# A sixth buffer for gated maps with eleven kept gelu results, a reordered mixing stage, and the next layer's first norm among the last V blocks

## The chip, the cores and the metric

One core of a Trainium2 chip runs the whole program. The metric is device time in microseconds, the median of several executions. TensorE is called PE here (its weight loads PEld), VectorE DVE, ScalarE ACT, GpSimd POOL, and SyncE SP; SP issues most of the transfers.

## What is computed

Two decoder layers over 512 tokens of 1024 channels, all float32. Each layer adds two sub-layers to x. The first mixes tokens with three groups of heads. The second, called PEER, picks for each token and each of eight heads 16 of 16384 experts and adds what they give:

```python
def reference(x, ...):
    for l in range(DEPTH):                       # DEPTH = 2
        xn = rms_norm(x, norm1_g[l])
        x = x + mixing_sublayer(xn, w_in[l], ..., w_out[l])
        xn = rms_norm(x, norm2_g[l])
        x = x + peer_ffn(xn, peer_wq[l], peer_keys[l], peer_u[l], peer_v[l])
    return x

# mixing: z = xn @ w_in, cut into three groups of heads
#   6 heads of stick-breaking attention (q, k normed), each head normed by out_g
#   6 heads of mLSTM (causal convolution and silu on q, k; input and forget gates), normed, times sigmoid(ml_o)
#   4 groups of spatial gating: gelu(u) * (w_s @ norm(gelu(v)) + b_s), normed;  result @ w_out
# PEER, for each token t:
sv, si = lax.top_k(scores, 16)                   # for each of the two half keys
best_s, best_p = lax.top_k(sums of pairs, 16);  gate = softmax(best_s);  idx = the pair's expert number
act = einsum('td,thkd->thk', xb, u_tab[ib])
y = einsum('thk,thkd->td', gelu(act) * gate, v_tab[ib])
```

## The kernel before

Tokens lie in four tiles of 128. PE works on float32 values split into a high and a low part (hi, lo), so that each product is three matmuls. A layer has these stages, and their times in layer 0 of the profiled execution are given for orientation.

**Mixing** (0 to about 330 us; function `mixing`). `norm_tiles` norms a tile of x (ACT squares and sums, `rsqrt_mean` takes Ln and Exp on ACT and some small DVE operations, DVE scales), and `to_channels` transposes it on PE and splits it into `xh` and `xl` on ACT and DVE. Then come the projections (`do_u`, `do_v`, `do_q`, `do_conv`, `do_mlv`, `do_og`), each with its weights loaded and split by `load_split`, and between them the heads (`sb_head`, `ml_head`), the spatial gating `sg_all`, the gate preparation `ml_prep`, the sigmoid of the output gate `og_sig`, the norm and transposition of the results `finish`, and the output projections `project_out`, which add to x. The order of the calls is written out (L570 to L614), but this part stands outside any manual schedule: a planner with its own costs may start an operation early where its operands and buffers are there. `act_set` preloads an activation table, and `tact` ties the activations that need it behind that load.

**PEER front** (to about 443 us; `peer_front`). Second norm, query projection, scores, and a top-16 search on DVE for each of the half keys. At its end `uprep(0)` splits the first block of u.

**Top-k, uact and gating** (443 to 823 us). From here the order on each engine is written by hand (`tc.manual_schedule`). The 16384 experts are 128 blocks of 128. For the first three tiles of tokens the kernel computes all of them: for each block e, `uact` multiplies u by x (24 matmuls, 128 x 384 each) and takes gelu. `uphase(e)` issues u_lo of block e+1 (DVE), the load of block e+4, u_hi of block e+2 (ACT) and then `uact(e)`. Results of blocks 0 to 59 (`NS`) are written to DRAM, the next ones (`NB`) are kept in SBUF. Beside that DVE runs `stage2`, the second top-k, tile by tile, and then the gating maps: for each of 24 batches of 16 tokens `make_maps(b, step)` makes two equality maps `oeq` (step 0; L900; two buffers) and three products `oag` of a map with a part of the gate (steps 1 to 3; L905; `AGB` = 5 buffers), and `quad(b, b4)` multiplies them on PE (12 small matmuls, L918) for four tokens at a time. `credit(w)` adds w to a balance and runs one `uphase` for each whole unit: `W_S` = 0.8 after each piece of `stage2`, `W_O` = 0.38 after each step of the maps. It stops at block `UB - 4` with `UB = NS + NB - 3`. The loop is

```python
for b in range(n_bat):
    for b4 in range(QB):
        quad(b, b4)
        make_maps(b + 1, b4)
        credit(W_O)
        gather((b * QB + b4) % 3 == 1)
```

The fourth tile (`NT - 1`) takes another way: `gather` fetches rows of u, then of v, by an indirect DMA on POOL and multiplies or adds them on DVE (L743, L754); there are 256 of these operations for a layer, spread over the gating and V stages.

**Tail and V stage** (823 to 1612 us). A short run of `uact` up to block `UB + 2`, then 128 V blocks: `vprep` multiplies gelu by the gate map and splits it and the block of v (wf, v_lo, wl on DVE; v_hi, wh on ACT), `vmm` adds 18 matmuls to six accumulators `ya`, which hold the result of three tiles. The remaining u blocks are interleaved, one to about two V blocks up to V block 120 (`UEND`). `spread(k, 252)` paces the gathers so that they end with step 252 of 256. After the last V block the six accumulators are added to x (L1042).

Layer 1 follows at once: its norm gains are loaded (L271), its first weights (L168), all four tiles are normed and transposed, and `do_u` takes the tiles in the order 0 to 3.

Of the kernel before, what the change touches and what calls it, by code (L numbers as in the profile page):

```python
# [17 lines left out]
P = 128  # L18
S = 512
# [22 lines left out]
NCH = TD // TC  # L42
GE = 4
GPAD = 128
NB = 13
NS = 60
UB = NS + NB - 3
W_S = 0.8
W_O = 0.38
G_R = 1  # L50
AGB = 5
UR = 3
G_B = 1
GBUF = 4
# [15 lines left out]
def trunk_kernel(ctx: ExitStack, tc: tile.TileContext, x, norm1_g, w_in, sb_qn_g, sb_kn_g, ml_conv_w,  # L70
# [56 lines left out]
    epoch = {"pre": None, "ops": []}  # L127
    no_sync = mybir.DependencyInfo(mybir.DependencyClass.NoSync, mybir.DependencyReason.SCHED_ONLY)

    def act_set(name):  # L130
        pre = nc.scalar.preload_act_table_set(name)
        for op in epoch["ops"]:
            tc.add_manual_dep(pre.ins, op.ins.name, no_sync, reason="table order")
        epoch["pre"], epoch["ops"] = pre, []

    def tact(out_ap, in_ap, func, **kw):
        op = nc.scalar.activation(out_ap, in_ap, func, **kw)
        tc.add_manual_dep(op.ins, epoch["pre"].ins.name, no_sync, reason="table order")
        epoch["ops"].append(op)
        return op  # L140

# [48 lines left out]
    def blocked(ap):  # L190
        return ap.rearrange("p (f c) -> p c f", c=ND)

    def to_channels(src, t, hi, lo, psp, perm=False):
        dst = slice(t * P, (t + 1) * P)
        cols = blocked(src) if perm else src.rearrange("p (c f) -> p c f", f=P)
        for d0 in range(0, ND, HALF):
            pt = psp.tile([P, S], F32, name="tr", bufs=1) if d0 else psp.tile([P, S], F32, name="zz", bufs=4)
            for d in range(HALF):
                nc.tensor.transpose(pt[:, d * P:(d + 1) * P], cols[:, d0 + d], ident)
            p3 = pt.rearrange("p (d t) -> p d t", t=P)  # L200
            sl = slice(d0, d0 + HALF)
            nc.scalar.activation(hi[:, sl, dst], p3, AF.Copy)
            nc.vector.tensor_sub(lo[:, sl, dst], p3, hi[:, sl, dst].bitcast(F32))
# [44 lines left out]
    def mixing(l, wst, fr, at, ps):  # L248
# [3 lines left out]
        with ExitStack() as yctx:  # L252
# [16 lines left out]
            if l == 0:  # L269
                load_x(0)  # L270
            nc.sync.dma_start(g1[:, :D], norm1_g[l][None, :].to_broadcast([P, D]))  # L271
            act_set(LOG_EXP)
            ws = [load_split(wst, w_in[l], C_UV, WG)]
            if l == 0:
                for t in range(1, NT):
                    load_x(t)
            ws.append(load_split(wst, w_in[l], C_UV + WG, WG))
            for t0 in range(NT):
                for t, xn in norm_tiles([t0], lambda: tmp("e", 1)[:, :D], lambda t: tmp("wt", 2)[:, :D],
                                        g1[:, :D]):  # L280
                    to_channels(xn, t, xh, xl, ps)
# [1 line left out]
            par, nm, bias_if, vn = load_params(l, ps)  # L283
            col = lambda key, i=0: par[:, nm[key] + i:nm[key] + i + 1]

            def natural(w, cw, evac):
                for t in range(NT):
                    pt = ps.tile([P, S], F32, name="mm", bufs=2)
                    mm3(pt[:, :cw], xp, w, lambda a, d: a[:, d, t * P:(t + 1) * P], lambda b, d: b[:, d, :])
                    evac(t, pt[:, :cw])  # L290

            def heads(pt, n):
                return pt.rearrange("p (h d) -> p h d", d=HD)
# [42 lines left out]
            def do_mlv(w):  # L336
                nc.gpsimd.memset(mlv[:, :, :, HD:HD + 1], 1.0)

                def evac(t, pt):
                    nc.vector.tensor_copy(mlv[:, t, :, :HD], heads(pt[:, :WM], HM))  # L340
                    nc.vector.tensor_add(ifn[:, t], pt[:, WM:].rearrange("p (a h) -> p a h", a=2), bias_if)

                natural(w, WM + 2 * HM, evac)

            def do_og(w):
                natural(w, WM, lambda t, pt: nc.scalar.activation(og[:, t, :], pt, AF.Copy))

            def do_u(w):
                natural(w, WG, lambda t, pt: nc.scalar.activation(uu[:, t, :], pt, AF.Copy))

            def do_v(w):
                natural(w, WG, lambda t, pt: nc.vector.tensor_copy(vv[:, t], heads(pt, GS)))
# [227 lines left out]
            do_conv(next_w(), 0)  # L580
            sb_head(1)
            do_conv(next_w(), 1)
            sg_all()
            sb_head(2)
            do_mlv(next_w())
            ml_prep()
            sb_head(3)
            sb_head(4)
            ml_head(0)
            sb_head(5)  # L590
            ml_head(1)
            do_og(next_w())
            og_sig()
            t_sb = mb.tile([P, 2, 3, S], F32R, name="yT_sb", tag="sqT")
            y_sb = (t_sb[:, 0], t_sb[:, 1])
            for c in range(3):
                finish(sbv, rsb, y_sb, c)
            ml_head(2)
            y_sg = (mb.tile([P, 2, S], F32R, name="yT_gh", tag="vv"),
                    yp.tile([P, 3, S], F32R, name="yT_gl", tag="sbv")[:, :2])  # L600
            u4 = uu.rearrange("p t (g d) -> p t g d", d=HD)
            for c in range(2):
                finish(u4, rsg, y_sg, c)
            project_out(y_sb, next_w(), 3, "mm", 2)
            ml_head(3)
            ml_head(4)
            project_out(y_sg, next_w(), 2, "mm", 2)
# [61 lines left out]
    def layer(l):  # L669
        with ExitStack() as pctx:  # L670
# [6 lines left out]
                    nc.sync.dma_start(uraw[e], peer_ut[l, e])  # L677

            def uprep_lo(e):
                if e in uraw:  # L680
                    src = uraw.pop(e)
                    nc.vector.tensor_sub(uT[e][1], src, uT[e][0].bitcast(F32))  # L682

# [9 lines left out]
            with ExitStack() as fctx:  # L693
                ps = fctx.enter_context(tc.tile_pool(name="ps_f", bufs=1, space=PSUM))
                wst = fctx.enter_context(tc.tile_pool(name="wst", bufs=1))
                mctx = ExitStack()
                fr = mctx.enter_context(tc.tile_pool(name="fr", bufs=1))
                at = mctx.enter_context(tc.tile_pool(name="at", bufs=1))
                mixing(l, wst, fr, at, ps)
                pr, xg, sbuf, svs, sis = peer_front(l, pctx, mctx, at, wst, ps, pools, uload)  # L700
                uprep(0)
            dr = pctx.enter_context(tc.tile_pool(name="dr", bufs=1, space=bass.MemoryType.DRAM))
            gd = dr.tile([NCH, P, NK * TC + GPAD], F32, name="gd")
            ge = dr.tile([NS, P, TD], F32, name="ge")
# [61 lines left out]
            def spread(k, n):  # L766
                if not left:
                    left.append(len(todo))
                gather(len(todo) - left[0] * max(0, n - k - 1) // n)

            with ExitStack() as bctx:
# [159 lines left out]
                        pace["credit"] -= 1  # L931

                with tc.manual_schedule():
                    uprep(1, lo=False)
                    uload(3)
                    for t in (NT - 1, *range(NT - 1)):
                        for _ in stage2(t):
                            credit(W_S)
                    casts = [f() for f in late]
                    credit(W_S)  # L940
                    for f in casts:
                        f()
                    tkctx.close()
                    with ExitStack() as octx:
                        oh = octx.enter_context(tc.tile_pool(name="oh", bufs=2))
                        stg = octx.enter_context(tc.tile_pool(name="stg", bufs=2))
                        for step in range(4):
                            make_maps(0, step)
# [7 lines that stand above are left out]
                u_tail = pace["e"]  # L956

            with ExitStack() as cctx:
# [26 lines left out]
                def vprep(k):  # L985
# [14 lines left out]
                    nc.vector.tensor_sub(wl, wf, wh.bitcast(F32))  # L1000
                    vT[e] = (wh, wl, vh, vl)

                def vmm(k):
                    e = order[k]
                    wh, wl, vh, vl = vT.pop(e)
                    for t in range(NT - 1):
                        tsl = slice(t * P, (t + 1) * P)
                        for half in range(2):
                            hs = slice(half * (D // 2), (half + 1) * (D // 2))
                            for i, (a, b) in enumerate(((wh, vh), (wh, vl), (wl, vh))):  # L1010
                                nc.tensor.matmul(ya[2 * t + half], a[:, tsl], b[:, hs],  # L1011
                                                 start=(k == 0 and i == 0), stop=(k == NK - 1 and i == 2))

                with tc.manual_schedule():
                    uprep_lo(u_tail + 1)
# [10 lines left out]
                    for k in range(NK):  # L1026
                        u_on = eu < NK and (k + 1) * (NK - NS - NB) >= (eu - NS - NB + 1) * UEND
                        vload(k + 2)
                        if u_on:
                            uload(eu + 4)  # L1030
                        vprep(k + 1)
                        spread(2 * k, 252)
                        if u_on:
                            uact(eu, ps, bufs=2)
                            uprep(eu + 2)
                            eu += 1
                        vmm(k)
                        spread(2 * k + 1, 252)
                for t in range(NT - 1):
                    for half in range(2):  # L1040
                        hs = slice(half * (D // 2), (half + 1) * (D // 2))
                        nc.vector.tensor_add(x_sb[:, t, hs], x_sb[:, t, hs], ya[2 * t + half])  # L1042

    for l in range(depth):
        layer(l)

# [35 lines left out]
```

## Time and profile before

| what | value |
|---|---|
| time, median of 3 executions (lowest to highest) | 3228.98 us (3225.39 to 3235.2) |
| the profiled execution, its own time | 3232.74 us |
| its span | 3231.0 us |
| mean granted clock of TensorE | 0.986 of full speed |
| busy in the span: PE, DVE, ACT, POOL | 3116.7, 2509.5, 1388.0, 681.5 us |
| DMA traffic | 748.49 MB, 232 GB/s on average, 320 GB/s in the V stage |

Busy times are those of one execution, in us or as a share of its span. PE's matmuls are pipelined, so a busy PE is not PE at its peak. "Idle before" is the time that an engine stood before an instruction, with the operation that ended that wait behind it. A line number stands for a line of the kernel; a helper's line is shared by all its callers, so the tile names tell them apart.

### The profile page before, as it was taken

To read this page: it belongs to the slowest core of one execution; us is meant where nothing else is said; L and a number is where in the kernel's file an instruction comes from. 1 tells how busy PE (TensorE), PEld (TensorE's weight loads), DVE (VectorE), ACT (ScalarE), POOL (GpSimd) and SP (SyncE) were. 2 spreads that over 40 slices of the span, in tenths; PEclk is the share of its full clock that TensorE was granted. 3 is DMA by queue.
4 is the path that set the end of the run, shared out by engine and by line. 5 is a ranking of instruction groups with operands and counts; after the bars stand their busy time and mean duration, and the time that the engine had idled before them with its cause. 6 is when DMAs were issued, how large, how long until landed. Compare 5 with 4: busy or idle time off the path is not lost.

```text
span 3231.0 us, 46311 instructions
## 1 busy us (share of the span) xinstructions
PE 3116.7 (96%) x17496; PEld 2776.7 (86%) x17496; DVE 2509.5 (78%) x4655; ACT 1388.0 (43%) x2002; POOL 681.5 (21%) x563
## 2 busy tenths in 40 slices
PE   8999999999999999999989999999999999999999
PEld 8877889998888888888887878899988888888888
DVE  4757889988677777877747578899886777778777
ACT  4553424566433333333355533345663333333333
POOL 1000000122233333333300000001212333333333
PEclk9999999999999999999999999999999999999999
DMA  4212325687999999999732123257879999999997
GB/s 141 68 33 61 102 70 176 232 291 264 337 331 324 324 332 316 334 330 323 252 107 67 34 60 101 75 186 242 289 262 322 328 329 321 332 318 336 328 324 264
DMA packets 329344, 748.49 MB, mean 232 GB/s; under 512 B 26404, under 2 KB 191328, under 8 KB 326048
## 3 DMA queue, kind: packets, MB, share of 16 engines
q1 hardware_dynamic: 233632, 401.76, 37.3%
q0 software_dynamic: 74752, 269.84, 23.9%
q10 hardware_dynamic: 20736, 73.93, 6.0%
q8 instruction: 137, 2.24, 0.3%
q14 instruction: 87, 0.71, 0.1%
HBM read 669.41 MB, written 76.02 MB: 231 GB/s over the span
## 4 chain that ended last, share of the span: by engine, by line
PE 85%; DVE 10%; ACT 3%; issue 2%; DMA 1%; SPq 0%; ACTq 0%; POOL 0%; DVEq 0%; POOLq 0%
PE y L1011 32%; PE act L714 26%; PE mm L187 13%; PE oh L918 4%; PE mm L533 3%; DVE u_lo L682 2%; DVE oag L905 1%; PE zz L367 1%; PE zz L653 1%; PE zz L467 1%; PE y L400 1%; PE y L478 1%; PE zz L392 1%; DVE bp L808 1%; DVE bp L805 1%
## 5 line engine op out<-in xcount | busy, mean ns | idle before, releaser
L714 PE MATMUL act<-xh,u_hi 128*128 128x384 f32 x2048 | 699.5, 342 | 6.4 <-ACT st L920 5.1
L714 PE MATMUL act<-xh,u_lo 128*128 128x384 f32 x2048 | 693.1, 338 | 11.2 <-DVE u_lo L682 11.2
L714 PE MATMUL act<-xl,u_hi 128*128 128x384 f32 x2048 | 693.0, 338 | 0.0
L1011 PE MATMUL y<-v_hi,wh 128*128 128x512 f32 x1536 | 599.9, 391 | 3.9 <-ACT wh L998 3.9
L1011 PE MATMUL y<-v_lo,wh 128*128 128x512 f32 x1536 | 599.6, 390 | 0.7 <-DVE v_lo L999 0.7
L1011 PE MATMUL y<-v_hi,wl 128*128 128x512 f32 x1536 | 598.7, 390 | 0.0
L997 ACT ACTIVATE v_hi<-v_raw 128x1024 fp32r<-128x1024 f32 x256 | 272.0, 1063 | 648.0 <-issue 575.5
L682 DVE TENSOR_TENSOR u_lo<-u_raw,u_hi 128x1024 fp32r<-128x1024 f32 x256 | 312.3, 1220 | 182.8 <-ACT u_hi L688 182.7
L999 DVE TENSOR_TENSOR v_lo<-v_raw,v_hi 128x1024 fp32r<-128x1024 f32 x256 | 312.9, 1222 | 160.8 <-ACT v_hi L997 160.8
L714 PEld LDWEIGHTS act<-xh,u_lo 128*128 128x128 f32 x2048 | 387.3, 189 | 13.6 <-DVE u_lo L682 13.3
L714 PEld LDWEIGHTS act<-xh,u_hi 128*128 128x128 f32 x2048 | 387.4, 189 | 11.4 <-ACT st L920 5.4
L714 PEld LDWEIGHTS act<-xl,u_hi 128*128 128x128 f32 x2048 | 387.2, 189 | 4.1
L740 POOL DMA_INDIRECT sbuf<-in_peer_u_dram,idx x128 | 170.8, 1334 | 1012.8 <-DVE sbuf L743 482.1
L717 ACT ACTIVATE gelu<-act 128x384 f32<-128x384 f32 x256 | 126.1, 492 | 521.7 <-PE act L714 521.6
L1011 PEld LDWEIGHTS y<-v_hi,wl 128*128 128x128 f32 x1536 | 289.2, 188 | 61.5 <-DVE wl L1000 0.7
L1011 PEld LDWEIGHTS y<-v_hi,wh 128*128 128x128 f32 x1536 | 288.8, 188 | 60.9 <-ACT wh L998 4.5
L1011 PEld LDWEIGHTS y<-v_lo,wh 128*128 128x128 f32 x1536 | 289.1, 188 | 57.0 <-DVE v_lo L999 1.3
L688 ACT ACTIVATE u_hi<-u_raw 128x1024 fp32r<-128x1024 f32 x256 | 271.7, 1062 | 37.0 <-ACT gelu L717 7.7
L740 POOL DMA_INDIRECT rows<-in_peer_u_dram,idx x128 | 165.5, 1293 | 365.9 <-DVE rows L743 354.1
L751 POOL DMA_INDIRECT sbuf<-in_peer_v_dram,idx x128 | 167.7, 1311 | 279.6 <-DVE x_sb L754 262.6
L920 ACT ACTIVATE st<-oh 128x512 f32<-128x512 f32 x192 | 198.6, 1141 | 46.6 <-PE oh L918 46.6
L751 POOL DMA_INDIRECT rows<-in_peer_v_dram,idx x128 | 159.3, 1245 | 280.0 <-DVE x_sb L754 246.4
(295 smaller groups left out, 5158.7 us busy)
## 6 DMA issues: line engine op xcount, KB each, us to landing
u_raw<-in_peer_ut_dram SPq DMA_DIRECT2D x256, 512.0 KB, 5.0
v_raw<-in_peer_v_dram SPq DMA_DIRECT2D x256, 512.0 KB, 6.5
gd<-st ACTq DMA_DIRECT2D x24, 2048.0 KB, 8.0
gt<-gd SPq DMA_DIRECT2D x64, 768.0 KB, 9.4
ge<-gelu ACTq DMA_DIRECT2D x120, 192.0 KB, 3.8
gelu_r<-ge SPq DMA_DIRECT2D x120, 192.0 KB, 6.1
w_raw<-in_w_in_dram SPq DMA_DIRECT2D x28, 768.0 KB, 4.4
w_raw<-in_peer_wq_dram SPq DMA_DIRECT2D x20, 768.0 KB, 5.5
```

The costliest lines, as they stand in the source:

```text
L187: nc.tensor.matmul(ps, a_sel(a[ah], d), b_sel(b[bh], d), start=(d == 0 and i == 0), stop=(d == n - 1 and i == 2))
L682: nc.vector.tensor_sub(uT[e][1], src, uT[e][0].bitcast(F32))
L688: nc.scalar.activation(uh, uraw[e], AF.Copy)
L714: nc.tensor.matmul(pa[:, :TD], a[:, d, :], b[:, d, :TD], start=(d == 0 and i == 0), stop=(d == ND - 1 and i == 2))
L717: nc.scalar.activation(gelu[e], pa[:, :TD], AF.Gelu_apprx_tanh)
L740: nc.gpsimd.indirect_dma_start(out=r, out_offset=None, in_=u_rows, in_offset=bass.IndirectOffsetOnAxis(ap=idx[:, p:p + 1], axis=0))
L751: nc.gpsimd.indirect_dma_start(out=r, out_offset=None, in_=v_rows, in_offset=bass.IndirectOffsetOnAxis(ap=idx[:, p:p + 1], axis=0))
L918: nc.tensor.matmul(pg[:, k, :], eq[:, 1, q, :, r], ag[i][:, q, :, r], start=(i == 0), stop=(i == 2))
L920: nc.scalar.activation(st[:, :, o:o + 4].rearrange("p i t -> p t i"), pg, AF.Copy)
L997: nc.scalar.activation(vh, vraw[e], AF.Copy)
L999: nc.vector.tensor_sub(vl, vraw.pop(e), vh.bitcast(F32))
L1011: nc.tensor.matmul(ya[2 * t + half], a[:, tsl], b[:, hs], start=(k == 0 and i == 0), stop=(k == NK - 1 and i == 2))
```

## The change

It has four parts. `AGB` goes from 5 to 6 and `NB` from 13 to 11, so that six products of maps can be in flight and 11 gelu results are kept. `uprep(1)` is moved from the beginning of the manual schedule to right behind `uprep(0)`, in the part that the planner orders, and with it its u_lo. In the mixing stage, `sg_all` comes after `ml_prep`, `finish` of the stick-breaking heads before `ml_head(1)`, `og_sig` after the first output projection, and the copy of the mLSTM values is made on ACT. Between the layers, the fourth tile of x, whose gathers now end with step 244 of 256, is normed for the next layer after V block 123 and transposed after V block 125; the table with Ln and Exp is loaded there and no more at the next layer's beginning; the accumulators are added to x tile by tile inside the last V block; and `do_u` of layer 1 begins with the fourth tile.

```diff
-NB = 13
+NB = 11
-AGB = 5
+AGB = 6
...
-    def act_set(name):
+    def act_set(name, manual=False):
         pre = nc.scalar.preload_act_table_set(name)
-        for op in epoch["ops"]:
+        for op in () if manual else epoch["ops"]:
             tc.add_manual_dep(pre.ins, op.ins.name, no_sync, reason="table order")
-        epoch["pre"], epoch["ops"] = pre, []
+        epoch["pre"], epoch["ops"], epoch["manual"] = pre, [], manual
...
-            act_set(LOG_EXP)
+            if l == 0:
+                act_set(LOG_EXP)
+            epoch["manual"] = False
...
-            for t0 in range(NT):
+            for t0 in range(NT if l == 0 else NT - 1):
...
-                    nc.vector.tensor_copy(mlv[:, t, :, :HD], heads(pt[:, :WM], HM))
+                    nc.scalar.activation(mlv[:, t, :, :HD], heads(pt[:, :WM], HM), AF.Copy)
...
-                natural(w, WG, lambda t, pt: nc.scalar.activation(uu[:, t, :], pt, AF.Copy))
+                natural(w, WG, lambda t, pt: nc.scalar.activation(uu[:, t, :], pt, AF.Copy),
+                        range(NT) if l == 0 else (NT - 1, *range(NT - 1)))
...
             do_conv(next_w(), 1)
-            sg_all()
             sb_head(2)
             do_mlv(next_w())
             ml_prep()
+            sg_all()
             sb_head(3)
             sb_head(4)
             ml_head(0)
             sb_head(5)
-            ml_head(1)
-            do_og(next_w())
-            og_sig()
             t_sb = mb.tile([P, 2, 3, S], F32R, name="yT_sb", tag="sqT")
             y_sb = (t_sb[:, 0], t_sb[:, 1])
             for c in range(3):
                 finish(sbv, rsb, y_sb, c)
+            ml_head(1)
+            do_og(next_w())
             ml_head(2)
...
             project_out(y_sb, next_w(), 3, "mm", 2)
+            og_sig()
             ml_head(3)
...
                 uprep(0)
+                uprep(1)
...
                 with tc.manual_schedule():
-                    uprep(1, lo=False)
                     uload(3)
...
+                def add_tile(t):
+                    for half in range(2):
+                        hs = slice(half * (D // 2), (half + 1) * (D // 2))
+                        nc.vector.tensor_add(x_sb[:, t, hs], x_sb[:, t, hs], ya[2 * t + half])
+
+                def ahead(k):
+                    t = NT - 1
+                    if k == NK - 10:
+                        nxt["g"] = vp.tile([P, D], F32, name="g_next", bufs=1)
+                        nc.sync.dma_start(nxt["g"], norm1_g[l + 1][None, :].to_broadcast([P, D]))
+                    elif k == NK - 5:
+                        act_set(LOG_EXP, manual=True)
+                        nxt["x"] = vp.tile([P, D], F32, name="x_next", bufs=1)
+                        for _ in norm_tiles([t], lambda: nxt["x"], lambda _: nxt["x"], nxt["g"]):
+                            pass
+                    elif k == NK - 3:
+                        to_channels(nxt["x"], t, xh, xl, ps, tags=(("act", 2), ("act", 2)))
...
+                        if k == NK - 1:
+                            add_tile(t)
...
-                        spread(2 * k, 252)
+                        spread(2 * k, 2 * NK - 12)
...
                         vmm(k)
-                        spread(2 * k + 1, 252)
-                for t in range(NT - 1):
-                    for half in range(2):
-                        hs = slice(half * (D // 2), (half + 1) * (D // 2))
-                        nc.vector.tensor_add(x_sb[:, t, hs], x_sb[:, t, hs], ya[2 * t + half])
-
+                        spread(2 * k + 1, 2 * NK - 12)
+                        if l + 1 < depth:
+                            ahead(k)
```

## Rows read from the trace of the kernel before

**Rows 1.** The page, busy us of each engine, share of span, instructions.

```profile
PE 3116.7 (96%) x17496; PEld 2776.7 (86%) x17496; DVE 2509.5 (78%) x4655; ACT 1388.0 (43%) x2002; POOL 681.5 (21%) x563
```

**Rows 2.** Stretches: length, busy PE, PEld, DVE, ACT, POOL, clock, DMA share, GB/s.

```profile
443.00:586.00 143.00, 134.20 (x736) 132.05 (x737) 136.81 (x462) 58.39 (x73) 4.06 (x4) 0.96 0.53 166
586.00:820.00 234.00, 217.92 (x1963) 210.56 (x1961) 207.45 (x213) 145.16 (x163) 48.55 (x31) 1.00 0.78 272
...
857.00:1610.00 753.00, 752.65 (x3614) 661.93 (x3614) 594.59 (x745) 270.46 (x363) 269.47 (x214) 1.00 0.92 320
```

**Rows 3.** Waits, whole span: who for whom, total us, times, longest us.

```profile
DVE oag L905 <- PE oh L918: 52.9, 38, 4.9
...
PE oh L918 <- DVE oag L905: 32.2, 28, 1.9
```

**Rows 4.** Timeline of PE in the gating stage: start, length, idle before.

```profile
656.07 0.73 PE L918 MATMUL oh<-oag,oeq 128*128 128x128 bf16 x10 [1.09 <-DVE oag L905]
...
675.63 0.73 PE L918 MATMUL oh<-oag,oeq 128*128 128x128 bf16 x10 [1.09 <-DVE oag L905]
...
820.03 2.93 PE L918 MATMUL oh<-oag,oeq 128*128 128x128 bf16 x48
```

**Rows 5.** Timeline of DVE in the same stretch of the gating stage.

```profile
654.79 1.23 DVE L905 TENSOR_TENSOR oag<-oeq,gateT 128x2048 bf16<-128x2048 bf16 x1 [1.27 <-PE oh L918]
655.94 2.35 DVE L900 TENSOR_TENSOR oeq<-iota_t,idxT 128x2048 bf16<-128x2048 bf16 x2
658.21 1.22 DVE L682 TENSOR_TENSOR u_lo<-u_raw,u_hi 128x1024 fp32r<-128x1024 f32 x1
659.34 1.22 DVE L743 SCALAR_TENSOR_TENSOR sbuf<-sbuf,xg 128x1024 f32<-128x1024 f32 x1
...
660.49 2.36 DVE L905 TENSOR_TENSOR oag<-oeq,gateT 128x2048 bf16<-128x2048 bf16 x2
```

**Rows 6.** Timeline of PE in the top-k stage, two of its stops.

```profile
453.12 0.69 PE L714 MATMUL act<-xh,u_lo 128*128 128x384 f32 x1 [4.79 <-DVE u_lo L682]
...
574.02 0.41 PE L868 MATMUL tr<-ident,ii 128*128 128x128 f32 x2 [1.62 <-DVE ii L852]
```

**Rows 7.** Timeline at the layer boundary: adds, weights, table, split, scaling, PE.

```profile
1609.22 2.73 DVE L1042 TENSOR_TENSOR x_sb<-x_sb,y 128x512 f32<-128x512 f32 x4 [1.43 <-PE y L1011]
...
1613.11 0.93 SPq L168 DMA_DIRECT2D w_raw<-in_w_in_dram  x2
...
1615.02 1.28 ACT L137 ACT_TABLE_LOAD   x1
1616.31 0.30 ACT L137 ACTIVATE rq_b<-rq_m 128x1 f32<-128x1 f32 x2
...
1619.07 1.04 ACT L173 ACTIVATE w_hi<-w_raw 128x1024 fp32r<-128x1024 f32 x1
...
1619.78 1.28 DVE L214 SCALAR_TENSOR_TENSOR wt<-x_sb,rs,sp 128x1024 f32<-128x1024 f32 x1
...
1621.16 1.09 PE L199 MATMUL zz<-ident,wt 128*128 128x128 f32 x4 [8.58 <-issue]
```

**Rows 8.** Stretches of the mixing stage and the layer boundary, as rows 2.

```profile
160.00:170.00 10.00, 7.72 (x32) 5.10 (x31) 7.80 (x18) 4.21 (x10) 0.00 (x0) 0.93 0.28 80
...
230.00:240.00 10.00, 7.72 (x41) 7.22 (x40) 6.55 (x11) 9.08 (x21) 0.00 (x0) 0.85 0.01 2
...
1612.60:1621.20 8.60, 0.04 (x1) 0.07 (x2) 2.96 (x10) 8.42 (x14) 0.14 (x2) 0.69 0.59 191
1621.20:1630.00 8.80, 7.09 (x32) 6.39 (x33) 6.07 (x16) 8.69 (x14) 0.00 (x0) 0.52 0.46 128
1630.00:1645.00 15.00, 12.75 (x104) 12.10 (x103) 8.31 (x12) 6.96 (x14) 0.00 (x0) 1.00 0.33 106
```

**Rows 9.** Groups by line, 185 to 260 (ACT) and 130 to 190 (DVE).

```profile
L154 ACT ACTIVATE sg<-og 128x384 f32<-128x384 f32 x4 | 2.1, 526 | 0.0
...
L543 DVE TENSOR_TENSOR vv<-vv,sgr 128x1024 f32<-128x1024 f32 x1 | 1.2, 1219 | 0.0
```

More of the change, by code (lines that the diff above doesn't have):

```diff
@@ L128, in trunk_kernel @@
     no_sync = mybir.DependencyInfo(mybir.DependencyClass.NoSync, mybir.DependencyReason.SCHED_ONLY)
-    def act_set(name):
+    def act_set(name, manual=False):
         pre = nc.scalar.preload_act_table_set(name)
-        for op in epoch["ops"]:
+        for op in () if manual else epoch["ops"]:
             tc.add_manual_dep(pre.ins, op.ins.name, no_sync, reason="table order")
-        epoch["pre"], epoch["ops"] = pre, []
+        epoch["pre"], epoch["ops"], epoch["manual"] = pre, [], manual
     def tact(out_ap, in_ap, func, **kw):
         op = nc.scalar.activation(out_ap, in_ap, func, **kw)
-        tc.add_manual_dep(op.ins, epoch["pre"].ins.name, no_sync, reason="table order")
+        if not epoch["manual"]:
+            tc.add_manual_dep(op.ins, epoch["pre"].ins.name, no_sync, reason="table order")
         epoch["ops"].append(op)
@@ L191, in blocked, with to_channels @@
         return ap.rearrange("p (f c) -> p c f", c=ND)
-    def to_channels(src, t, hi, lo, psp, perm=False):
+    def to_channels(src, t, hi, lo, psp, perm=False, tags=(("zz", 4), ("tr", 1))):
         dst = slice(t * P, (t + 1) * P)
@@ L196, in to_channels @@
         for d0 in range(0, ND, HALF):
-            pt = psp.tile([P, S], F32, name="tr", bufs=1) if d0 else psp.tile([P, S], F32, name="zz", bufs=4)
+            name, bufs = tags[d0 // HALF]
+            pt = psp.tile([P, S], F32, name=name, bufs=bufs)
             for d in range(HALF):
@@ L284, in mixing, with natural @@
             col = lambda key, i=0: par[:, nm[key] + i:nm[key] + i + 1]
-            def natural(w, cw, evac):
-                for t in range(NT):
+            def natural(w, cw, evac, tiles=range(NT)):
+                for t in tiles:
                     pt = ps.tile([P, S], F32, name="mm", bufs=2)
@@ L679, in uprep_lo @@
             def uprep_lo(e):
-                if e in uraw:
+                if e in uraw and e in uT:
                     src = uraw.pop(e)
@@ L1001, in vprep @@
                     vT[e] = (wh, wl, vh, vl)
+                def add_tile(t):
[14 more added lines that the diff above has]
+                        to_channels(nxt["x"], t, xh, xl, ps, tags=(("act", 2), ("act", 2)))
+                nxt = {}
                 def vmm(k):
```

## The prediction

> **What bounds the kernel now.** I read the page first, then the busy times by stretch, then the list of waits, then the order of instructions where a wait repeats. The page says that TensorE is busy for 96% of the span [rows 1], so a gain has to come out of the remaining 4%, or out of stretches in which its clock is low. The stretches show where those lie [rows 2]: in the V stage PE is busy for 752.65 of 753 us, so nothing can be won there and all PE work moved into it is paid in full. In the gating stage (586 to 820, its twin of layer 1 is alike) PE is idle for 16 of 234 us, while DVE is busy for 207. The list of waits names it [rows 3]: PE waits 28 times, 32.2 us in all, for a gate product (oag), and DVE waits 38 times, 52.9 us, for PE to give an oag buffer back. Each waits for the other, which is what too few buffers look like. The order on PE shows the rhythm [rows 4]: every second batch PE stops for 1.09 us in its first quad; from one stop to the next it is 19.56 us. On DVE the third product of the next batch is only made when PE has ended the batch before [rows 5].
>
> **The change part by part.** All sums are against the profiled execution, 3232.7 us with a span of 3231.0; the median of the timed runs, 3229.0, is 3.7 lower, and I carry the difference over to it unchanged.
>
> *Sixth map buffer.* With five buffers the third product of batch b+1 waits for the last quad of batch b. With six it waits for nothing that is recent. The next limit is oeq with two buffers: the first map of batch b+1 may start when quad 3 of batch b-1 has ended. From there DVE has to do two maps (2.27 us start to start), three products of 1.15, and its share of u_lo (1.13) and gather products (1.15) [rows 5]. Until PE needs the result, five credit calls of 0.38 pass, 1.9 uact blocks, and four quads; four quads take 2.93 us [rows 4] and a block 4.1 (two batches hold 8 quads and about 3 blocks: 19.56 - 1.09 - 5.9 = 12.6, by three). So PE has 2.9 + 1.9 x 4.1 = 10.7 us, DVE needs 2.27 + 3.45 + 1.9 x 1.13 + 1.33 x 1.15 = 9.4. DVE mostly comes in time; where only one block falls in between (about one batch in ten) it is 7.0 against 8.4 and PE waits 1.4. I leave 2.4 such waits, 3 us, in each layer: -32.2 + 6 = **-26**. Over two batches DVE has 17.9 us of work and PE 18.5, so the stage stays PE's, by 0.6 us.
>
> *Two fewer kept results (NB 13 to 11).* The cap on blocks in this stage falls from 66 to 64. 37 credit calls of 0.8 bring 29.6 blocks, then come four calls of 0.38 and one after each quad: the last block comes after quad 87 of 96 instead of quad 92. The two blocks go to the V stage (57 instead of 55 there), where PE pays the same 4.1 us: zero. Their DVE part, two u_lo, goes where DVE is busy 595 of 753 us [rows 2]: zero. But the last batch now has no block over it: PE has four quads (2.9 us), DVE from the release of oeq on 2.27 + 3.45 + 1.15 = 6.9, so PE waits about 3.9 us. Before, the last four quads ran without a stop [rows 4]. **+7.8** for two layers. If the clock falls after this wait too, about 3 us more a layer: idle PE at the layer boundary is followed by 8.8 us at a granted clock of 0.52 [rows 8], and this wait is half as long. I take none of it, and keep +6 as the bound.
>
> *uprep(1) ahead of the top-k stage.* PE's longest stop in that stage is 4.79 us for u_lo [rows 6]. The edit moves one u_lo to where DVE is less busy, but the next u_lo stands behind the same top-k work, and DVE is busy 136.8 of 143 us there [rows 2]. At 574 PE again waits for DVE (1.62 us) [rows 6], so whatever PE wins at the start it gives back there, except DVE's own saving of one operation: 1.13 us a layer, **-2.3**, at least 0, at most the full 9.6.
>
> *Next layer's first norm.* This counts once. Now PE ends V at 1612.6 and stands 8.58 us [rows 7]; then come 8.8 us at clock 0.52 with 1.7 us of gaps, and 2.25 us of gaps until 1645 [rows 8]. The adds of x are no part of it: four of them already run from 1609.22, under the last matmuls [rows 7]. The weights are asked for at 1613.11, when V's buffers come free, and ACT splits them at 1619.07 [rows 7]; tile 3 being ready in advance, PE waits for that load instead: 0.5 us to the issue, at most 6.0 to the split and I take 5 (ACT was busy too), 1.04 for the split, so 6.5 in place of 8.6. ACT loses its seven table loads of 1.28 us, 9.0 in all [rows 7], since one load now stands in the last V blocks; I count half of the 4 us of gaps for it. The clock falls either way. -2.1 - 2.0 = -4.1. The transposes of tile 3 move into V at their price: zero. In block 123 the norm's chain (square, Ln, Exp on ACT, 1.28 us of scaling on DVE [rows 7]) stands ahead of the preparation of a later block, which has the length of one V block to be ready in: 753 us less 55 uact blocks of 4.1 is 128 times 4.1. It has little to spare: +0.5, bounds 0 and 4.1. The norm weights are one more 512 KB on the SP queue among v loads, which are buffered three deep: zero. The gathers end four blocks earlier, 3% more of them per block, under DVE's 158 us of slack [rows 2]: zero. **-3.6**.
>
> The Trainium skill ("ScalarE: Activation LUTs", What ACT_TABLE_LOAD costs) gives a switch of set 1283 ns and a drain of about 1380 more. Here the activation behind a load starts 0.01 us after it [rows 7], so I see no drain; by the page the seven loads would be 18.6 us.
>
> *Mixing order.* finish of the stick-breaking heads comes before ml_head(1) and do_og, so its transposes have some 16 us of matmuls (do_og's 96 at 0.17, a 24th of a uact block) to hide in; now PE is idle for 2.3 us at 230 to 240 and its clock is 0.85 [rows 8]. sg_all goes behind ml_prep; now PE is idle for 2.3 us in 160 to 170 at 0.93 [rows 8]. og_sig goes behind the first projection, and the copies of mlv go from DVE to ACT; both engines are half idle. A planner orders this stage, so new stops can appear anywhere. At best both stops and their clock go, 4.6 + 2.2 = 6.8 a layer; at worst others replace them. I take 4 a layer, **-8**, bounds -14 and +8.
>
> Sum: -26 + 7.8 - 2.3 - 3.6 - 8 = **-32**: 3200.6 for the profiled execution, **3197** for the median.
>
> **The rivals.**
> DVE takes over the gating stage. It has 17.9 us of work in each 18.5; 5% slower operations make 18.8, and with 0.3 for uneven batches 19.1, 0.6 over PE, in 12 pairs of batches and two layers: +15, 3212. For it: DVE's load; against it: its 52.9 us of waiting are there to be used [rows 3]. The Trainium skill ("Perfetto Trace Analysis", Identifying the Most-Contended Engine) would judge PE by weight loads rather than matmuls: 210.6 us against DVE's 207.5 [rows 2], which makes this rival look nearer.
>
> The sixth buffer isn't the one that was missing: DVE then waits for oeq at the same place, the 26 us stay and the 7.8 are paid: -6, 3223. Against it: DVE's listed waits in this stage are all before oag, none before oeq.
>
> ACT's loads set the boundary: then all 9.0 us come off it and not 3.6: -5.4, 3192. For it: PE starts behind ACT's chain; against it: the weights' load ends late anyway. The rule of the skill above would make this still more.
>
> Slower: the new mixing order lays bare what it moves. og_sig is 16 activations of 0.52 us, 8.4 us, on ACT ahead of ml_head(3), and sg_all begins with three DVE operations of 1.22, 3.7 us, ahead of sb_head(3) [rows 9]. If PE has nothing else then, it stands 12.1 us a layer and loses about 6 more to the clock, as after the boundary [rows 8]: 36 in both, with the 8 not gained: -32 + 8 + 36 = +12, 3241. It outweighs the rest once two thirds of it are bare. Against it: around these places PE is busy nearly all the time, and projections are there to fill.
>
> **How the numbers follow.** Forecast 0.62 (3182 to 3209 by itself: the bounds of the mixing order and of the boundary, not all at once), DVE as the bound 0.14, ACT's loads 0.08, no effect 0.09, slower 0.07. A measurement of this kernel tells about 0.3%, 10 us, from no change. Faster by more than that: the forecast, DVE and ACT, 0.84; the same: 0.09; slower: 0.07. The range 3179 to 3216 takes in the first three, with the falling clock and the mixing bounds, and leaves out the last two.
>
> **What would show it.** PE's waits for oag fall from 28 to about five and DVE's busy share in the gating stage rises from 89% towards 95%; a new wait of about 4 us stands before the last batch; the first wait for u_lo comes one block later and is shorter, and the wait at the turn of tile 2 is longer; no table loads after the last V block, and PE idle of 6 to 7 us there; the 2.3 us stops at the stick-breaking finish are gone. I am wrong if the waits before quads stay, if V gets PE idle time, or if the mixing stage changes by more than 14 us.

## The result and the profile after

The changed kernel takes 3204.2 us (median of five; 3199.8 to 3212.8) where the kernel before, timed beside it, takes 3228.0: a ratio of 0.9933 with a 95% interval of 0.9918 to 0.9948, 0.7% faster. The forecast was 3197 us, with a range of 3179 to 3216. (One execution of a later run, g2, took 6182.6 us and stands in no figure below.) The profiled execution of the changed kernel has a span of 3206.5 us, against 3231.0.

The page, busy us of each engine (answers [rows 1]):

```profile
PE 3123.8 (97%) x17496; PEld 2782.4 (87%) x17496; DVE 2506.4 (78%) x4647; ACT 1383.3 (43%) x2004; POOL 677.6 (21%) x563
```

PE does the same 17496 matmuls, but is busy 7 us longer than before. So the span became 24.5 us shorter although matmuls took longer somewhere, and that is a matter of clock: the mean granted clock is 0.981, where it was 0.986. The list of waits, columns as in [rows 3]:

```profile
DVE oeq L906 <- PE oh L924: 20.5, 16, 3.1
PE oh L924 <- DVE oag L911: 11.5, 10, 2.0
...
PE tr L513 <- DVE dg L510: 4.3, 2, 2.2
```

PE's waits for gate products fall from 28 to 10 (forecast about five) and from 32.2 to 11.5 us; DVE no longer waits for an oag buffer at all, but for oeq, the next limit that the prediction named. The last line is new: a stop in the stick-breaking finish. Stretches, columns as in [rows 2]; 591 to 806 is the gating stage up to its last quad, the second line is the V stage:

```profile
591.00:806.00 215.00, 209.21 (x1937) 202.91 (x1936) 204.51 (x212) 144.20 (x162) 50.02 (x32) 0.99 0.82 293
840.00:1604.00 764.00, 763.73 (x3676) 672.41 (x3677) 601.96 (x756) 276.69 (x374) 267.05 (x214) 1.00 0.91 318
```

DVE is busy for 95% of the gating stretch (89% in [rows 2]), and PE idles 5.8 us of 215 where it idled 16 of 234. V stays full. Two thirds of the remaining waits stand at one place per layer, here on the timeline of PE:

```profile
800.26 0.23 PE L924 MATMUL oh<-oag,oeq 128*128 128x128 bf16 x1 [1.99 <-DVE oag L911]
801.39 0.22 PE L924 MATMUL oh<-oag,oeq 128*128 128x128 bf16 x1 [0.90 <-DVE oag L911]
802.53 1.71 PE L924 MATMUL oh<-oag,oeq 128*128 128x128 bf16 x17 [0.92 <-DVE oag L911]
```

That is the last batch, which has lost its U blocks: 3.8 us, forecast 3.9. The layer boundary, stretches as in [rows 8] and then the table loads on ACT's timeline from 1603 to 1622:

```profile
1604.90:1610.70 5.80, 0.08 (x2) 0.06 (x1) 3.08 (x14) 5.19 (x13) 0.14 (x2) 0.80 0.75 241
1610.70:1620.00 9.30, 9.30 (x62) 9.24 (x63) 8.85 (x13) 6.19 (x10) 0.00 (x0) 0.76 0.52 149
1620.00:1630.00 10.00, 9.59 (x80) 9.34 (x80) 2.82 (x5) 4.24 (x8) 0.00 (x0) 1.00 0.51 159
```

```profile
1608.77 0.20 ACT L137 ACTIVATE rs<-rq_b 128x1 f32<-128x1 f32 x1
...
1609.78 1.28 ACT L131 ACT_TABLE_LOAD   x1
1611.08 1.06 ACT L174 ACTIVATE w_hi<-w_raw 128x1024 fp32r<-128x1024 f32 x1
```

PE idles 5.72 us instead of 8.58 (forecast 6.5), has 0.4 us of gaps afterwards instead of 4.0, and 9.3 us at 0.76 instead of 8.8 us at 0.52. Of the seven table loads one is left here, for gelu; forecast was none. The mixing stage of layer 0, stretches:

```profile
230.00:240.00 10.00, 9.64 (x55) 7.39 (x54) 5.31 (x9) 6.79 (x13) 0.00 (x0) 1.00 0.34 107
240.00:250.00 10.00, 7.16 (x20) 4.61 (x20) 6.56 (x24) 4.36 (x16) 0.00 (x0) 0.65 0.00 0
250.00:260.00 10.00, 10.00 (x32) 7.04 (x31) 4.57 (x14) 2.41 (x8) 0.00 (x0) 0.50 0.00 1
260.00:270.00 10.00, 10.00 (x47) 7.88 (x46) 4.84 (x16) 2.73 (x9) 0.00 (x0) 0.82 0.01 2
```

The stop of [rows 8] at 230 to 240 has become one at 240 to 250, and behind it the granted clock is at the lower level (0.50 is 1.2 GHz) for some 20 us, through the second slice and into the third while PE is fully busy. The first U block of layer 0 starts at 446.85 instead of 443.52. The mixing stage thus lost time, where the forecast had -8.

### The profile page after: what moved, and what is told of

Read it like the earlier page. It is cut to its first block, busy times and chain, and to the rows that moved or that the text cites. A ratio compares the mean times of both kernels' runs of the same rounds, so it can differ in the third digit from the quotient of the medians.

```text
span 3206.5 us, 46330 instructions
## 1 busy us (share of the span) xinstructions
PE 3123.8 (97%) x17496; PEld 2782.4 (87%) x17496; DVE 2506.4 (78%) x4647; ACT 1383.3 (43%) x2004; POOL 677.6 (21%) x563
```

## The experiments

The theory after the result (A): the buffers and the boundary give more than forecast, and the new mixing order costs some 9 us through the clock. Rival: the terms of the prediction hold, and the missing 7 us are somewhere else. In what follows "old order" means the changed kernel with the mixing stage as it was.

**Buffers and cap by themselves.**

```diff
# e1_six_cap11, from the kernel before       # e2_cap11: the first line alone
-NB = 13
+NB = 11
-AGB = 5
+AGB = 6
```

> The kernel before with only the two sizes of the gating stage changed: six buffers for gated maps, 11 kept gelu results. Theory A, from the trace after: the gating stages lost 10.7 and 14.9 us beside the two U blocks that left each of them, the V stages gave 0.8 back, so this alone is worth about -25 us: 3203, nearly all of the change's gain. Theory B, the terms of the prediction: -26 + 7.8 = -18, so 3210, and the rest of the gain comes from the other edits.

> The kernel before with only the cap of kept gelu results lowered from 13 to 11; five buffers stay. Theory A, the prediction's term: the last block comes before quad 88 instead of 93, which opens waits of 3.9 us per layer, and the two U blocks moved among the V blocks cost nothing: +8, 3236. Rival: those two blocks, 4.3 us each, also covered the wait for a buffer in the gating stage; with five buffers every one of their microseconds is waited again, +17, 3245. Second rival: with five buffers the queue before the last blocks is no shorter than before, so nothing changes: 3228.

Measured: e1 3205.1 us, ratio 0.9927 (0.9913 to 0.9941); e2 3237.7, ratio 1.0030 (1.0021 to 1.0038). PE's and DVE's waits for each other, e2 first, then e1:

```profile
DVE oag L905 <- PE oh L918: 48.0, 34, 4.1
PE oh L918 <- DVE oag L905: 39.1, 34, 1.9
```

```profile
DVE oeq L900 <- PE oh L918: 16.7, 15, 2.4
PE oh L918 <- DVE oag L905: 11.4, 10, 2.0
```

The cap alone costs 9.3 us (forecast 7.8), of which 6.9 are waits. The sixth buffer on top of it is worth 32.5 (forecast 26). Its waits fall by 27.7 us; from the first quad to the first V matmul the two layers take 247.9 and 248.2 us in e1 against 264.0 and 265.5. The stage times decide for A: 16.1 and 17.3 us a layer, where the prediction's term is 13. By the median alone e1 lies 2 us above A's 3203 and 5 below B's 3210. In e2 the prediction's term for the cap fits, and its two rivals (3245 and 3228) don't.

**The preparation of block 1 ahead of the top-k stage.**

```diff
# h1_six_uprep, from e1
-                if e in uraw:
+                if e in uraw and e in uT:
...
 uprep(0)
+uprep(1)
...
-                    uprep(1, lo=False)
```

> Six buffers and the lower cap (3205.1) with the second U block's preparation moved ahead of the top-k stage; no other edit. Theory: the wait for u_lo at the second block falls from 4.79 to 3.08 us in layer 0 and as much in layer 1, and nothing else moves: -3, 3202. Rival: the wait comes back at a later block, 3205. With it, the old mixing order in the changed kernel (3194.4) differs from this by the next layer's first norm alone: -8 by the traces, -3.6 by the prediction.

Measured: 3205.6 us, ratio 0.9936 (0.9923 to 0.9950), against 3205.1 for e1: nothing. PE's timeline in e1, then in h1:

```profile
449.64 0.69 PE L714 MATMUL act<-xh,u_lo 128*128 128x384 f32 x1 [4.79 <-DVE u_lo L682]
...
570.54 0.41 PE L868 MATMUL tr<-ident,ii 128*128 128x128 f32 x2 [1.63 <-DVE ii L852]
```

```profile
452.98 0.69 PE L715 MATMUL act<-xh,u_lo 128*128 128x384 f32 x1 [3.08 <-DVE u_lo L682]
...
570.27 0.41 PE L869 MATMUL tr<-ident,ii 128*128 128x128 f32 x2 [1.62 <-DVE ii L853]
```

The stop is 1.7 us shorter, yet from the first U block to the first quad h1 takes 144.3 us and e1 143.8. The rival, that it comes back, fits. The stop at the turn of tile 2 is no longer than before (1.63 and 1.62), but the granted clock behind it differs, in e1 and then in h1:

```profile
570.00:580.00 10.00, 9.21 (x53) 9.00 (x54) 9.79 (x16) 2.72 (x4) 0.00 (x0) 1.00 0.39 121
```

```profile
570.00:580.00 10.00, 9.47 (x46) 9.26 (x47) 9.79 (x16) 2.25 (x3) 0.00 (x0) 0.83 0.36 111
```

That is 9.47 x 0.17 = 1.6 us of clock, about what the shorter stop had won; in layer 1 h1 has 0.83 as well (2170 to 2180) and e1 1.00. Where the clock stays up there, in f2 below, these stretches take 142.9 and 142.7 us, 1 us less than in e1 (143.8 and 143.9).

**The mixing order off, and alone.** e3_after_oldmix takes the hunk of the mixing stage and the copy on ACT out of the changed kernel; e4_mix_only puts just these into the kernel before.

> The changed kernel with the mixing stage in its old order (and the mLSTM value copy back on DVE). Theory A, from the two traces (first U block at 446.85 instead of 443.52 in layer 0, and 416.4 instead of 410.4 us from the end of the first projection to it in layer 1): the new order costs 3.3 + 6.0 = 9 us, so without it 3195, faster than the changed kernel by 0.3%. Rival, the prediction's term: the new order is worth -8, so without it 3212.

> The kernel before with only the mixing stage reordered and the value copy on ACT. Theory A: the stop of 2.15 + 0.69 us ahead of the stick-breaking projection is followed by some 20 us at the lower clock, now that the og projection no longer stands before it, so +3 in layer 0 and +6 in layer 1: 3237. Rival, the prediction: -8, 3220. If it gives 3228, the 9 us of the new mixing order that the traces show belong to another edit that reaches into that stage.

Measured: e3 3194.4 us, ratio 0.9891 (0.9873 to 0.9908); e4 3239.6, ratio 1.0021 (1.0006 to 1.0035), its runs from 3226.6 to 3244.1. By the medians the order costs 9.8 us in the one and 11.3 in the other (6.8 by e4's ratio), and e3 is faster than the changed kernel. A holds. But the loss is not there in every execution. e4's twelve line up with their mean granted clocks: 0.987 in the two fastest (3226.6 and 3227.1), which are no slower than the kernel before (3228.4), 0.981 in the five from 3239.5 to 3241.2, 0.980 in the two slowest. e3 and h1 differ by the next layer's first norm alone: 11.2 us between the medians.

**Which of the moves.**

```diff
# f5_old_early_finish, from e3
+for c in range(3):
+    finish(sbv, rsb, y_sb, c)
 ml_head(1)
 do_og(next_w())
 og_sig()
-for c in range(3):
-    finish(sbv, rsb, y_sb, c)
# f2_old_ogsig_late, from e3
 do_og(next_w())
-og_sig()
...
 project_out(y_sb, next_w(), 3, "mm", 2)
+og_sig()
# f1_after_finish_back: the changed kernel with the finish after do_og, the reverse of f5's edit
```

> The old mixing order in the changed kernel (3194.4) with the early stick-breaking finish alone. Theory A: all of the loss comes with it, 3204, with a stop of about 2 us on the finish's dg and 20 us at the lower clock. Rival: the finish alone costs nothing, 3194, and the loss needs og_sig behind the projection as well.

> The old mixing order in the changed kernel (3194.4) with og_sig alone moved behind the stick-breaking projection. The prediction's step on its own: the 2.28 us stop on yT_sb per layer goes, and some of the clock behind it: -5 to -7, 3189. Rival: og_sig's 24 instructions lie under work where they stood, the stop is set by the finish's own chain, so 3194; second rival: they now stand between the projection and the mLSTM heads that PE waits for, +4, 3198.

> The changed kernel with one line group moved back: the three stick-breaking finishes stand again behind the fourth-last mLSTM head and the og projection; og_sig and sg_all stay late, the value copy stays on ACT. Theory A: the early finish is what costs 10 us, since the dense og projection now runs before the last stick-breaking head instead of under its finish; then 3194, and if the late og_sig also does what the prediction said, 3189. Rival: one of the other moves (og_sig, sg_all, the copy on ACT) costs the 10 us, so it stays at 3204.

Measured: f5 3194.1 us, ratio 0.9897 (0.9882 to 0.9912); f2 3188.2, ratio 0.9883 (0.9868 to 0.9898); f1 3197.8, ratio 0.9911 (0.9896 to 0.9926). So the late og_sig is worth 6 us, as expected of f2: f5, timed together with f2, takes as long as e3, and their executions don't overlap with f2's. f1 lies between its two theories. The same stretch in e3 and in f2:

```profile
230.00:240.00 10.00, 7.73 (x37) 6.42 (x37) 6.61 (x12) 8.90 (x21) 0.00 (x0) 0.83 0.08 29
```

```profile
230.00:240.00 10.00, 8.43 (x47) 6.20 (x45) 8.12 (x14) 9.88 (x24) 0.00 (x0) 1.00 0.28 75
```

The early finish alone costs nothing in f5, against A, though it makes the very stop that the changed kernel has. PE's timeline in f5, then in the changed kernel:

```profile
243.03 1.56 PE L472 MATMUL zz<-cqk 64*128 64x384 f32 x6
246.74 1.12 PE L513 MATMUL tr<-ident,dg 128*128 128x128 f32 x4 [2.15 <-DVE dg L510]
...
254.04 2.00 PE L483 MATMUL y<-mlv,wt 128*128 128x65 f32 x16
```

```profile
238.97 1.56 PE L472 MATMUL zz<-cqk 64*128 64x384 f32 x6
242.68 0.78 PE L513 MATMUL tr<-ident,dg 128*128 128x128 f32 x4 [2.15 <-DVE dg L510]
...
251.47 3.67 PE L483 MATMUL y<-mlv,wt 128*128 128x65 f32 x16
```

Same work, same stop; 7 to 9 us behind it, sixteen matmuls take 2.00 us in the one and 3.67 in the other. f5's clock is 0.76 and 0.90 in the slices 240 to 260, where the changed kernel has 0.65 and 0.50. So the stop isn't the loss; how long the clock stays down is.

**The other moves on top of the best.** All four start from f2.

```diff
# g1_ogsig_sgall_late
-sg_all()
 sb_head(2)
 do_mlv(next_w())
 ml_prep()
+sg_all()
# g2_ogsig_late_mlv_act
-                    nc.vector.tensor_copy(mlv[:, t, :, :HD], heads(pt[:, :WM], HM))
+                    nc.scalar.activation(mlv[:, t, :, :HD], heads(pt[:, :WM], HM), AF.Copy)
# g4_ogsig_late_early_finish: the edit of f5
# g3_ogsig_late_wo352
-W_O = 0.38
+W_O = 0.352
```

> The old mixing order in the changed kernel with og_sig late (3188.2), and sg_all moved behind ml_prep as well. The changed order with the finish put back (3197.8) differs from 3188.2 by this move and the copy on ACT. Theory: sg_all's move is the one that costs the 9.6 us, by TensorE's clock and not by waits (its stop on dg of 0.7 us a time goes): 3198. Rival, the prediction: the stop goes and nothing else happens, -2 to -4: 3185.

> The old mixing order in the changed kernel with og_sig late (3188.2), and the mLSTM value copy on ACT instead of DVE. Theory: eight copies of some 0.6 us change engines under do_mlv's matmuls and nothing waits for them: 3188. Rival: ACT delivers them later than DVE did and the heads wait, or the clock falls there; then this is the 9.6 us: 3198.

> The old mixing order in the changed kernel with og_sig late (3188.2), and the early stick-breaking finish as well. Theory: the early finish brings back the stop of 2.15 + 0.69 us per layer that the late og_sig had taken away, and 3 us at the lower clock: +8, 3196, which undoes the gain of og_sig's move. Rival: the pair is what holds the clock low for 20 us, as in the changed kernel: 3204. Second rival: 3188, no interaction.

> The old mixing order in the changed kernel with og_sig late (3188.2), and the U blocks of the gating stage spread thinner: 0.352 credits per quad instead of 0.38, so that the last block comes after quad 93 or 94 instead of 87; their number is the same. Theory: the waits of 3.8 us per layer in the last batch stood there only because no block was left to cover DVE: they go, -6 to -8, 3181. Rival: one batch of elementwise work per 8 quads is all that DVE can do with 0.38 blocks per quad, so with fewer blocks per quad the waits come back in the earlier batches and sum to the same: 3188.

Measured: g1 3183.0 us, ratio 0.9861 (0.9843 to 0.9880); g2 0.9853 (0.9830 to 0.9876), in runs of 3178.7, 3179.1 and 3185.3 us; g4 3200.9, ratio 0.9904 (0.9885 to 0.9923), runs from 3193.0 to 3205.6; g3 3192.4, ratio 0.9895 (0.9878 to 0.9912). So sg_all's move and the copy on ACT cost nothing by themselves and seem worth 5 and 9 us by the medians (3183.0 and 3179.1 against 3188.2), though the intervals overlap with f2's. Yet f2 with both is f1, and f1 takes 9.6 us more than f2: the moves don't add up. g1's theory, that sg_all's move is what costs, falls. g1's stretch 160 to 170 (of [rows 8]) has no idle time left:

```profile
160.00:170.00 10.00, 10.00 (x68) 9.65 (x67) 5.72 (x12) 3.93 (x9) 0.00 (x0) 1.00 0.00 1
```

g4 is the telling one. Its time follows the clock too, from 3193.0 us at 0.989 to 3205.6 at 0.984, and the profile is of the slowest execution; its median lies between its theory (3196) and its rival (3204). This one execution of one kernel has the same stop (2.15 and 0.69 us) in both layers, at 248.21 and at 1846.38; the stretches around the first and around the second:

```profile
240.00:250.00 10.00, 7.05 (x39) 4.98 (x37) 4.47 (x20) 4.12 (x12) 0.00 (x0) 0.90 0.25 80
250.00:260.00 10.00, 9.99 (x28) 7.08 (x28) 4.86 (x11) 3.27 (x12) 0.00 (x0) 0.50 0.00 1
260.00:270.00 10.00, 10.00 (x39) 7.74 (x39) 4.16 (x12) 1.74 (x6) 0.00 (x0) 0.57 0.00 0
```

```profile
1842.00:1852.00 10.00, 7.17 (x28) 5.33 (x28) 5.59 (x22) 4.01 (x15) 0.00 (x0) 0.68 0.01 2
1852.00:1862.00 10.00, 10.00 (x59) 7.72 (x59) 6.82 (x18) 3.19 (x10) 0.00 (x0) 0.98 0.00 0
1862.00:1872.00 10.00, 10.00 (x43) 7.38 (x43) 7.27 (x21) 3.60 (x12) 0.00 (x0) 1.00 0.00 0
```

In layer 0 the low clock takes 10.0 us (busy time by one minus the clock: 0.7 + 5.0 + 4.3), in layer 1 2.5. As time at 0.50 that is some 20 us in layer 0 (10 x (0.10 + 0.50 + 0.43) / 0.50) and some 7 in layer 1. f1, without the early finish, shows the same without any long stop. Its PE has the same two short idle times in both layers, 0.94 us and, 7 us later, 0.35; the clock fell behind them in layer 1 alone. Layer 0, and then layer 1:

```profile
236.00:246.00 10.00, 9.65 (x58) 6.95 (x56) 6.34 (x21) 4.87 (x16) 0.00 (x0) 1.00 0.21 70
246.00:256.00 10.00, 9.69 (x54) 7.42 (x54) 7.92 (x23) 4.20 (x13) 0.00 (x0) 1.00 0.00 1
```

```profile
1820.00:1830.00 10.00, 9.65 (x50) 6.86 (x48) 6.76 (x14) 7.11 (x18) 0.00 (x0) 0.88 0.31 106
1830.00:1840.00 10.00, 10.00 (x30) 6.84 (x30) 3.35 (x19) 1.30 (x6) 0.00 (x0) 0.50 0.01 2
```

g3, whose last block comes later, fits its rival: it moves the waits without removing them: 12 of at most 1.0 us instead of 10 of at most 2.0, the same sum (f2 has 11.5), and gating stages of 247.7 and 247.5 us (f2: 248.1 and 247.7):

```profile
PE oh L924 <- DVE oag L911: 11.0, 12, 1.0
DVE oeq L906 <- PE oh L924: 9.6, 14, 1.6
```

## Why the prediction was right, and where it wasn't

The time fell inside the range that was forecast, and the mechanism of the largest term is confirmed. But the terms were off in both directions: the mixing order missed by 17.8 us, the sixth buffer and the norm by 14.1 the other way. That the sum came within 8 us is luck. By the differences of the medians:

| term | forecast | measured | from |
|---|---|---|---|
| sixth buffer | -26 | -32.5 | e1 against e2 |
| cap 13 to 11 | +7.8 | +9.3 | e2 against before |
| uprep(1) | -2.3 | +0.5, nothing | h1 against e1 |
| next layer's first norm | -3.6 | -11.2 | e3 against h1 |
| mixing order | -8 | +9.8 | changed kernel against e3 |
| sum | -32 | -24 | |

The column adds up by construction, since each row compares neighbours in one chain from the kernel before to the changed one. The runs come from several sessions, in which the kernel before had medians of 3227.2 to 3230.4; by the ratios instead the last two terms are -14.5 and +13.6, so each is known to some 4 us.

*Sixth buffer and cap.* The mechanism was right in detail: oeq is the next limit, DVE reaches 95%, the last batch waits 3.8 us, two short waits are left elsewhere in each layer (1.9 us; forecast 3). The listed waits explain 27.7 of the 32.5. Most of the rest is clock, which the prediction named for the cap, with +6 as a bound, and took as nothing: behind the waits of the last batch e2 loses 6.4 us to it (0.86 and 0.80 in the slices from 806 to 826, 0.71 and 0.77 from 2420 to 2440), e1 2.8 (0.83 from 790 to 800, 0.66 from 2388 to 2398, 1.00 in the slice after each). The rivals "DVE takes over" and "not the one that was missing" fall; the first was near, since with thinner U blocks (g3) waits come in earlier batches.

*uprep(1).* The stop moved by one block and shrank by 1.7 us, as forecast; that DVE's own saving arrives at the end did not happen in h1, where the clock at the turn of tile 2 took it back. The prediction looked for a longer wait there, and the wait is the same.

*The boundary.* The trace gives the size apart from the mixing stage behind it: the stop -2.9 (5.72 against 8.58; forecast -2.1), the gaps -3.6 (0.4 against 4.0; forecast half of them, -2.0), the low clock -2.0 (9.3 x 0.24 = 2.2 against 8.8 x 0.48 = 4.2; forecast none), and tile 3's transposes, which V now carries, about +1. That is -7.5, twice the term. The step that failed is "the clock falls either way": it falls for a shorter time after a shorter stop. Counting half of the gaps failed too: nearly all of them went. The runs' 11.2 fits: counted from the last V matmul, PE in e3 is 9.0 us ahead of PE in h1 some 28 us on, and 1.7 of the other 2.2 are clock in a place that the edit doesn't touch (h1 has 0.90 and 0.93 from 1690 to 1710, e3 1.00). The rival in which all of ACT's loads come off (9.0 us) is nearer in size than the forecast; no run takes the loads off by themselves, so its mechanism is not shown. The Trainium skill's price for all seven ("ScalarE: Activation LUTs", What ACT_TABLE_LOAD costs) would be, as an estimate, 18.6 us; neither the 7.5 nor the 11.2 reaches it, and the load that is left is again followed by the next activation after 0.02 us. The hiccup in block 123 didn't come: PE idles 0.3 us in 764.

*Mixing order.* This is the term that failed: +9.8, about its upper bound of +8, where -8 was forecast. Three of the four moves gain or cost nothing when they are tried singly (f2, g1, g2). The early finish did not do what was said, for two reasons. The first is the reading of the old stop. In the kernel before, the transposes of the finish already ran without a wait:

```profile
232.83 0.60 PE L508 MATMUL tr<-ident,dg 128*128 128x128 f32 x4
...
234.65 0.52 ACT L137 ACTIVATE sg<-sg 128x384 f32<-128x384 f32 x1
...
235.06 0.59 ACT L510 ACTIVATE yT_sb<-tr 128x512 fp32r<-128x512 f32 x1
...
235.71 0.50 PE L533 MATMUL mm<-w_hi,yT_sb 128*128 128x512 f32 x1 [2.28 <-ACT yT_sb L510]
```

PE waited for ACT's copy of their result, and ACT was busy with og_sig's operations (sg) and a head's until then. Moving og_sig alone, in f2, halves the stop to 1.15 us. The second reason is that "its transposes have some 16 us of matmuls to hide in" took program order for PE's order. In the changed kernel do_og's matmuls run at 204.6 to 211.8 and 224.4 to 229.0, ahead of the last stick-breaking head, whose products end at 239.03; behind that head come only six 64-row matmuls (1.56 us), while the finish needs 3.6 us of small DVE and ACT steps before the first transpose. So a stop of 2.15 + 0.69 us replaces one of 2.3. That alone is a draw. What makes it dear is the clock behind it, which stays low for 20 us in the light matmuls of the mLSTM heads. Not shown is why the clock of the changed kernel, of e4 and of g4's layer 0 stays low that long and f5's doesn't, nor that it is the early finish alone that brings it about. Taking it back gains 6.4 us (f1) and adding it to f2 costs 12.7 (g4), but f1 does without it and has some 17 us at the lower level in layer 1, and e4's fastest executions have it and are no slower than the kernel before. The slower rival, that og_sig and sg_all lie bare, is refuted: neither move costs time by itself.

The version that beats both kernels is f2 with one more move, g1 or g2: some 1.4% below the kernel before and 0.7% below the changed one. Both together are f1, at 3197.8, with the low clock in layer 1 of its profile.

## What to carry to other kernels

Where two engines wait for each other's buffers, one more buffer can take off more than the listed waits (here 32.5 us for 27.7), and the next limit can be read in advance by asking what the faster engine will wait for then. Where a planner orders an engine, read the order that it made before counting on a neighbour in the program as cover. A change made of several moves should be timed move by move and also together: here moves that gain singly lose together, and one kernel's executions differ by up to 17 us with the clock, so a single profile doesn't tell what an order costs.

## What the runs showed of the hardware

After the same stop in the same work, TensorE's granted clock was low for about 7 us or for about 20 (g4, layers 1 and 0), which is 2.5 or 10 us of time per place; and it fell to 0.50 for a fully busy stretch of 64-row and 65-column matmuls with idle times of only 0.94 and 0.35 us in the 11 us before (f1, layer 1), while the same work with the same idle times kept 1.00 in layer 0. The spread of such kernels shows it: e4's twelve runs cover 17.5 us, at mean granted clocks from 0.987 down to 0.980, and f2's four cover 4.2, at 0.990 and 0.989.
